# A merged run of small recurrence products in the second layer, and exponentials two steps later

## The chip, the cores and the metric

The kernel runs on one core of a Trainium2 chip. A core has five engines with their own instruction streams: TensorE (PE in the profile; its weight loads are PEld), VectorE (DVE), ScalarE (ACT), GpSimd (POOL) and SyncE (SP, which here only issues DMAs). The metric is the device time of one execution in microseconds, as a median of the runs.

## The reference

Two layers of a decoder trunk over 256 tokens of width 1024. Each layer projects the normalised tokens into ten groups of 512 columns, runs three branches, gates their outputs, and projects them back with a residual:

```python
for l in range(DEPTH):
    h = rms_norm(x, norm_g[l])
    q_a, k_a, v_a, q_h, f_h, i_h, q_m, z = jnp.split(h @ w_in[l], split_points, axis=-1)
    o_a = moba_attention(qa, ka, va)                      # 8 heads x 64, causal, own block of 256 keys
    o_h = hgrn2_chunkwise(q_h, f_h, i_h, lb_all[l])       # 4 heads x 128, gated linear recurrence
    o_m = memory_attention(qm, km, vm)                    # 4 heads x 128, over 256 memory tokens
    x = x + (jnp.concatenate([o_a, o_h, o_m], -1) * jax.nn.silu(z)) @ w_out[l]
```

The change touches the recurrence. Its score of query t on an earlier key s is a sum over 128 channels d of

```python
scores = jnp.einsum('bhtd,bhtsd,bhsd->bhts', qc, decay, kc)   # decay = product of the forget gates from s+1 to t
```

## The kernel before

**The stream of weights.** All projections are one chain of matmuls over 120 chunks of weights (128 x 1024 floats). A chunk is loaded by SP into `wr`, rounded on ScalarE into `wh` (L143), and the remainder `wr - wh` is formed on VectorE into `wl` (L158); each product is three matmuls (`wh` by the high part, `wh` by the low part, `wl` by the high part) into an `acc` bank. Loads run five chunks ahead of TensorE, `wh` four, `wl` two (`DMA_AHEAD`, `H_AHEAD`, `L_AHEAD`). Chunks of kind B give 12 matmuls of 512 columns, chunks of kind A 24 of 256 columns.

**The side work.** Everything else is written as generators (`g_...`), which `spawn` puts on a list. `slot`, called once per half chunk, advances each by one step; `yield n` makes one sleep n steps. Side work on TensorE writes to four `sd` banks, counted by `room`/`rel`. So the step number sets where an instruction stands in the program; a list scheduler of the framework then moves instructions within what data, buffers and pins allow. Each engine executes its own list in order.

**The recurrence (`g_hgrn`).** The decay of a pair (t, s) is built up in levels: level 1 pairs neighbours, level 2 pairs of two, then 4, 8, 16, 32, 64. For each channel a tree of forget products is kept (`Tm`, halved by `up`), queries `Q` and keys `K` are multiplied level by level by the forget products on their way to the middle of the pair (`mul`, L799), and the products of a level are then plain matmuls of 32 x 32 blocks, 32 of them, over the 128 channels. `row` issues such a run of 32 (L202): K block as weights, up to 48 columns of `QX` as moving operand, into one `sd` bank. Each product is fp32 and takes two passes, so a run of 32 is 64 records in the profile. Three runs are made for each layer: `low` (the diagonal and level 1, from `QX0`, `K0`), one for levels 2 and 4 (at m = 2) and one for levels 8 and 16 (at m = 8). `put` copies the parts of a bank that a level owns into `hSd` with a mask (`COPY_PREDICATED`, L796). Before, `low` is made beside the run of m = 2 and all use one pair of tiles, `QX` (`hQ`) and `K` (`hK`), which the next level overwrites in place. Levels 32 and 64 follow with runs of 16 and 8 products.

**The attention group.** `g_qk` transposes keys and queries (L993), casts them into `k2` (two tiles, with buffer tags `k2` and `y2`) and copies halves of them by DMA from ScalarE's queue (L1005). `g_moba_unit` (u = 0, 1) makes scores, maxima, sleeps four steps, takes exponentials on ScalarE (L1059, pinned in program order), scales them on VectorE (L1068), transposes `P` on TensorE (L1078, pinned) and copies it into `PT` (L1079). ScalarE's exponential and sigmoid are in different function sets: between them stands an `ACT_TABLE_LOAD`. Sigmoids `sg` of the gate (L732) come in the same part of the layer.

## Time and profile before

| | |
|---|---|
| median of 3 runs | 396.51 us (396.29 to 396.57) |
| the profiled execution | 396.15 us, span from first to last instruction 394.4 us |
| granted TensorE clock | 1.000 |
| VectorE and ScalarE busy | 315.3 us and 251.0 us |
| first layer's recurrence runs on TensorE | from 70.6 us on |
| second layer's, before the change | from 255.9 us on |
| DMA, mean | 180 GB/s |

A row of a timeline gives the start in us from the first instruction, the duration, the engine, the line, the operation with its output and input tiles, the shape, and how many alike stand in the row (x). On TensorE durations overlap, since matmuls are pipelined: the pace is read from start to start. `sd` and `acc` are PSUM banks. A row of a group (by line and form) gives the count, then the busy time in us, and the mean of one in ns. A row of waits gives who waited for whom: us in total, times, the longest.

### The profile page before, as it was taken

Reading aid. Unit: us, or ns where it says so; the run is one execution under the profiler, and the core shown is the slowest. Engines: PE = TensorE matmul, PEld = TensorE weight load, DVE = VectorE, ACT = ScalarE, POOL = GpSimd, SP = SyncE. Lnnn points to the kernel's source line nnn. Section 1 sums busy time; section 2 is a strip of 40 time slices with the busy share of each in tenths; the row PEclk is TensorE's granted clock in tenths of the full one; section 3 lists DMA queues with packets and bytes.
Section 4 is the critical chain, followed back from the end, with each engine's and each line's share of the span. In section 5 each row is a group of like instructions: output and inputs, shape, how many; then the busy total and the mean of one; then the engine's idle time right before and its main releaser. Section 6 shows DMA issues by size and latency. Waiting matters only on the chain.

```text
span 394.4 us, 7907 instructions
## 1 busy us (share of the span) xinstructions
PE 390.2 (99%) x3052; PEld 353.4 (90%) x3052; DVE 315.3 (80%) x628; ACT 251.0 (64%) x401; POOL 66.4 (17%) x94
## 2 busy tenths in 40 slices
PE   9999999999999999999999999999999999999996
PEld 6789988888999888999988999888889998899996
DVE  5799988999998748776586999799998684588563
ACT  6788776439687579644463785535865974968330
POOL 2007734430001002000061040033300200200000
DMA  8998654558544453533646375637665266444203
GB/s 274 419 349 303 198 198 144 162 158 234 197 161 157 165 191 131 157 111 111 209 161 212 124 237 181 209 108 227 193 193 172 73 197 200 140 158 161 81 27 108
DMA packets 22661, 70.92 MB, mean 180 GB/s; under 512 B 2528, under 2 KB 5984, under 8 KB 22624
## 3 DMA queue, kind: packets, MB, share of 16 engines
q1 hardware_dynamic: 19872, 67.86, 51.6%
q10 hardware_dynamic: 2752, 2.56, 2.4%
q8 instruction: 24, 0.39, 0.4%
q14 instruction: 13, 0.11, 0.1%
HBM read 67.27 MB, written 1.05 MB: 173 GB/s over the span
## 4 chain that ended last, share of the span: by engine, by line
PE 94%; DMA 3%; SPq 0%; ACT 0%; DVE 0%; POOL 0%; issue 0%; DVEq 0%; ACTq 0%
PE acc L198 60%; PE acc L1225 17%; PE sd L198 10%; DMA zT<-in_x_dram 2%; PE sd L202 2%; PE sd L1099 1%; PE sd L1078 1%; PE sd L993 1%; DMA mw<-in_front_dram 1%; PE sd L1187 1%; PE sd L633 0%; PE sd L1133 0%; PE sd L767 0%; SPq L123 0%; ACT sqx L446 0%; PE sd L423 0%
## 5 line engine op out<-in xcount | busy, mean ns | idle before, releaser
L143 ACT CAST wh<-wr 128x1024 fp32r<-128x1024 f32 x104 | 109.0, 1052 | 76.2 <-PE acc L198 44.2
L158 DVE TENSOR_TENSOR wl<-wr,wh 128x1024 fp32r<-128x1024 f32 x104 | 126.8, 1224 | 31.3 <-PE acc L198 11.3
L198 PE MATMUL acc<-wh,hT 128*128 128x512 f32 x384 | 120.5, 391 | 0.0
L198 PE MATMUL acc<-hT,wh 128*128 128x256 f32 x512 | 91.4, 280 | 0.0
L198 PEld LDWEIGHTS acc<-wh,hT 128*128 128x128 f32 x384 | 72.0, 188 | 14.7
L198 PEld LDWEIGHTS acc<-hT,wh 128*128 128x128 f32 x512 | 78.2, 188 | 0.2
L198 PE MATMUL acc<-wl,hT 128*128 128x512 f32 x192 | 75.5, 393 | 0.0
L198 PE MATMUL acc<-hT,wl 128*128 128x256 f32 x256 | 70.9, 279 | 0.0
L198 PEld LDWEIGHTS acc<-hT,wl 128*128 128x128 f32 x256 | 47.9, 188 | 0.1
L198 PEld LDWEIGHTS acc<-wl,hT 128*128 128x128 f32 x192 | 36.1, 188 | 7.3 <-DVE wl L158 0.2
L1225 PE MATMUL acc<-yh,wl 128*128 128x256 f32 x128 | 35.7, 280 | 0.0
L1225 PE MATMUL acc<-yl,wh 128*128 128x256 f32 x128 | 35.3, 277 | 0.0
L1225 PE MATMUL acc<-yh,wh 128*128 128x256 f32 x128 | 35.0, 278 | 0.0
L1225 PEld LDWEIGHTS acc<-yl,wh 128*128 128x128 f32 x128 | 24.1, 188 | 0.1
L1225 PEld LDWEIGHTS acc<-yh,wl 128*128 128x128 f32 x128 | 24.1, 188 | 0.0
L1225 PEld LDWEIGHTS acc<-yh,wh 128*128 128x128 f32 x128 | 23.8, 188 | 0.1
L161 DVE SCALAR_TENSOR_TENSOR wl<-wr,gT,wh 128x1024 fp32r<-128x1024 f32 (+1 forms) x14 | 18.8, 1355 | 4.9 <-PE acc L198 2.0
L1225 PE MATMUL acc<-y,wh 128*128 128x256 f32 x128 | 21.8, 276 | 0.0
L148 ACT ACTIVATE wh<-wr,gT 128x1024 fp32r<-128x1024 f32 (+1 forms) x14 | 15.2, 1089 | 10.4 <-PE acc L198 3.6
L1225 PEld LDWEIGHTS acc<-y,wh 128*128 128x128 f32 x128 | 19.2, 188 | 0.0
L1059 ACT ACTIVATE P<-P,nba,rq 128x128 f32<-128x128 f32 (+1 forms) x32 | 17.2, 539 | 0.9 <-DVE nba L1050 0.8
L1225 PE MATMUL acc<-y,wl 128*128 128x256 f32 x64 | 17.5, 276 | 0.0
(246 smaller groups left out, 669.3 us busy)
## 6 DMA issues: line engine op xcount, KB each, us to landing
wr<-in_w_in_dram SPq DMA_DIRECT2D x80, 512.0 KB, 3.7
wr<-in_w_out_dram SPq DMA_DIRECT2D x24, 512.0 KB, 3.2
wr<-in_w_mem_kv_dram SPq DMA_DIRECT2D x12, 512.0 KB, 3.4
k<-k ACTq DMA_DIRECT2D x8, 256.0 KB, 5.3
zT<-in_x_dram SPq DMA_DIRECT2D x2, 512.0 KB, 9.4
xs<-in_x_t_dram SPq DMA_DIRECT2D x2, 512.0 KB, 9.8
memr<-in_mem_dram SPq DMA_DIRECT2D x2, 512.0 KB, 4.9
mw<-in_front_dram SPq DMA_DIRECT2D x2, 384.0 KB, 4.8
```

The source lines that it names most:

```text
L143: ins = nc.scalar.copy(whs[i], raws[i])
L148: nc.scalar.activation(whs[i][:, sl], raws[i][:, sl], AF.Copy, scale=gT[:, g:g + 1])
L158: nc.vector.tensor_tensor(wls[i], raws[i], whs[i].bitcast(F32), op=OP.subtract)
L161: nc.vector.scalar_tensor_tensor(wls[i][:, sl], in0=raws[i][:, sl], scalar=gT[:, g:g + 1], in1=whs[i][:, sl].bitcast(F32), op0=OP.mult, op ...
L198: nc.tensor.matmul(o, lhsT=a, rhs=b, start=s, stop=e)
L202: tc.keep_in_program_order(nc.tensor.matmul(o, lhsT=a, rhs=b, start=True, stop=True))
L993: nc.tensor.transpose(pt[:, p * 128:(p + 1) * 128], kr[:, t, p * 128:(p + 1) * 128], ident)
L1059: pin(nc.scalar.activation(P[:, i, kc[t]], P[:, i, kc[t]], AF.Exp, bias=nb[:, c:c + 1], scale=rq[:, r:r + 1], accum_out=sm[:, c:c + 1]))
L1078: pin(nc.tensor.transpose(pt[:, i * 128:(i + 1) * 128], P[:, i, bs], ident))
L1099: pin(nc.tensor.matmul(po[w][rows, c + o:c + 256], lhsT=va[:, b, h * 64:(h + 1) * 64], rhs=PT[e][:, p, 256 * b:256 + 128 * b], start=b == ...
L1187: nc.tensor.transpose(pt[:, i * 256 + t * 128:i * 256 + (t + 1) * 128], P[:, t, i, b * 128:(b + 1) * 128], ident)
L1225: ins = nc.tensor.matmul(a, lhsT=wt, rhs=y, start=first and (to is not None or b % 2 == 0), stop=n == nk - 1 and j == 2, skip_group_check= ...
```

## The change

It touches the second layer (l = 1) alone.

1. In `g_hgrn`, queries and keys of levels 1 to 4 get tiles of their own, `hQ2` and `hK2`, in the buffers of tags `y2` and `k2`. At m = 2 no run is issued; the halves of keys and queries that the level leaves as they are go by two copies on ScalarE into `hK` and `hQ`, the others are multiplied into them. At m = 8, when three banks are free, the three runs (m = 8, m = 2, `low`) are issued together: 96 products, 192 passes. The masked writes of all three follow after that level's multiplications.
2. In `g_moba_unit`, the sleep ahead of the exponentials is 6 steps in place of 4, for both u.

The first layer goes through the same code with one run of `low` and m = 2, and one of m = 8, as before.

```diff
+        QX2, K2 = QX, K
+        if l:
+            QX2 = sb.tile([128, 32, 64], F32, name="hQ2", tag="y2", bufs=1)
+            K2 = sb.tile([128, 1024], F32, name="hK2", tag="k2", bufs=1)
+        Q2 = QX2[:, :, 0:32]
...
-        def up(m, src=K):
+        def up(m, src=K, dst=K):
...
-        nc.scalar.copy(pairs(K, 1)[:, :, 1], pairs(K0, 1)[:, :, 1])
+        nc.scalar.copy(pairs(K2, 1)[:, :, 1], pairs(K0, 1)[:, :, 1])
...
-        up(1, K0)
-        for m in (2, 8):
+        up(1, K0, K2)
+        first, todo = True, []
+        for m, QXm, Km in ((2, QX2, K2), (8, QX, K)):
+            todo.append((m, QXm, Km))
...
-            yield from room("sd", 2 if m == 2 else 1)
-            g, gs = row(K, lambda c: QX[:, c].rearrange("p (n x) -> p n x", x=4 * m)[:, :, m:])
-            if m == 2:
-                low = row(K0, lambda c: QX0[:, c])[1]
-            yield 2
...
+            rows = []
+            if m == 8 or not l:
+                yield from room("sd", len(todo) + first)
+                for n, a, k in todo[::-1]:
+                    rows.insert(0, (n, row(k, lambda c: a[:, c].rearrange("p (n x) -> p n x", x=4 * n)[:, :, n:])[1]))
+                todo = []
+                if first:
+                    low = row(K0, lambda c: QX0[:, c])[1]
+                yield 2
+                if first:
+                    rel("PTh")
+                    rel("PTl")
+                    put_low(low)
+                    rel()
+                first = False
+            else:
+                nc.scalar.copy(pairs(K, 2)[:, :, 1], pairs(K2, 2)[:, :, 1])
+                nc.scalar.copy(Qn[:, :, :, 0, 0], Qv[:, :, :, 0, 0])
+                yield 4
+            mul(Qn[:, :, :, 0, 1], Qv[:, :, :, 0, 1], Tq[:, :, :, 0, 0])
+            for v in range(2):
+                mul(Qn[:, :, :, 1, v], C[:, :, :, v], Tq[:, :, :, 0, 0])
+            up(m, Km)
+            up(2 * m)
+            for n, g in rows:
...
-        yield 4
+        yield (6 if l else 4)
```

Two places show what this does to the order.

TensorE, before, around the second layer's runs: first the run of m = 2 with `low`, where `hQ`, `hK` are the current tiles and `hQ_2965`, `hK_2814` are `QX0`, `K0`:

```order
L198 MATMUL acc<-wh,hT 128x512
L202 MATMUL sd<-hQ,hK 32x48 x32
L202 MATMUL sd<-hQ_2965,hK_2814 32x48 x32
L198 MATMUL acc<-wh,hT 128x512
L198 MATMUL acc<-wl,hT 128x512
```

and 56 matmuls of 512 columns later the run of m = 8, with eight transposes of keys behind it:

```order
L198 MATMUL acc<-wh,hT 128x512 x3
L202 MATMUL sd<-hQ,hK 32x48 x32
L993 MATMUL sd<-ident,kr 128x128 x8
L198 MATMUL acc<-wl,hT 128x512
L198 MATMUL acc<-wh,hT 128x512
```

After the change, 44 such matmuls behind the old place of the first run, `hQ_3055` and `hK_3056` being `hQ2` and `hK2`:

```order
L198 MATMUL acc<-wh,hT 128x512
L202 MATMUL sd<-hQ,hK 32x48 x32
L202 MATMUL sd<-hQ_3055,hK_3056 32x48 x32
L202 MATMUL sd<-hQ_2965,hK_2814 32x48 x32
L198 MATMUL acc<-wl,hT 128x512
L198 MATMUL acc<-wh,hT 128x512
L198 MATMUL acc<-wl,hT 128x512
L198 MATMUL acc<-wh,hT 128x512
L1009 MATMUL sd<-ident,kr 128x128 x4
L198 MATMUL acc<-wh,hT 128x512
```

The two runs have become one, and the transposes of keys come in two blocks of four, the first 8 matmuls ahead of the old place of the eight and the second 11 behind it.

ScalarE, before, around the exponentials of u = 0 in the second layer (`P,sma_3569`; `sq` is a square for the recurrence's output norm, `sg` a gate sigmoid, `wh` a weight chunk):

```order
L732 ACTIVATE sg<-acc 128x512
L1059 ACT_TABLE_LOAD
L1059 ACTIVATE P,sma_3569<-P,nba_3568,rq 128x256 x2
L589 ACTIVATE sq<-sd 128x512
L1059 ACTIVATE P,sma_3569<-P,nba_3568,rq 128x128 x2
L589 ACTIVATE sq<-sd 128x512
L1059 ACTIVATE P,sma_3569<-P,nba_3568,rq 128x128 x2
L143 CAST wh<-wr 128x1024 x2
L1059 ACTIVATE P,sma_3569<-P,nba_3568,rq 128x256 x2
L732 ACT_TABLE_LOAD
L732 ACTIVATE sg<-acc 128x512
```

And after, from the first `sq` on:

```order
L1075 ACT_TABLE_LOAD
L1075 ACTIVATE P,sma_3569<-P,nba_3568,rq 128x128 x2
L143 CAST wh<-wr 128x1024
L589 ACTIVATE sq<-sd 128x512
L1075 ACTIVATE P,sma_3569<-P,nba_3568,rq 128x128 x2
L1075 ACTIVATE P,sma_3569<-P,nba_3568,rq 128x256 x2
L143 CAST wh<-wr 128x1024
L732 ACT_TABLE_LOAD
L732 ACTIVATE sg<-acc 128x512
L143 CAST wh<-wr 128x1024
L1075 ACT_TABLE_LOAD
L1075 ACTIVATE P,sma_3569<-P,nba_3568,rq 128x256 x2
```

The last two exponentials now come behind a gate sigmoid and one more weight chunk, so the set of functions changes twice more. TensorE's transposes of this `P` move back by 35 matmuls of 256 columns. SP's and GpSimd's lists are unchanged.

## The prediction

> **What bounds the kernel now.** I read the page first, then the waits of TensorE alone, then the chain of waits, then the timelines of the second layer's recurrence.

> ```profile
> PE 390.2 (99%) x3052; PEld 353.4 (90%) x3052; DVE 315.3 (80%) x628; ACT 251.0 (64%) x401; POOL 66.4 (17%) x94
> PE 94%; DMA 3%; SPq 0%; ACT 0%; DVE 0%; POOL 0%; issue 0%; DVEq 0%; ACTq 0%
> ...
> PE sd L198 <- PEq L1361: 0.8, 1, 0.8
> PE sd L423 <- DVE dg L418: 0.2, 1, 0.2
> PE sd L198 <- ACT wh L148: 0.2, 1, 0.2
> ```

> TensorE is busy 99% of the span and 94% of the chain is its own. The lower three rows are all its waits: 1.2 us in 394.4, none on an operation that the change touches. So a gain must come out of TensorE's own stream, a loss must be a gap in it, and a microsecond taken from or given to another engine counts only where TensorE comes to wait for it.

> A busy TensorE is not always at its pace, so I need the pace. The chain of waits has two long unbroken stretches:

> ```profile
> 272.22 8.21 PE acc L198 x36
> ...
> 305.49 11.13 PE acc L198 x98
> ```

> That is 0.228 us for a matmul of 512 columns and 0.1136 us for one of 256. Against it the timeline shows what a run of small products costs at its edges:

> ```profile
> 255.58 0.39 PE L198 MATMUL acc<-wh,hT 128*128 128x512 f32 x1
> 255.90 1.57 PE L202 MATMUL sd<-hQ,hK 128*32 128x48 f32 x128
> 257.39 0.50 PE L198 MATMUL acc<-wh,hT 128*128 128x512 f32 x1
> 257.73 0.40 PE L198 MATMUL acc<-wl,hT 128*128 128x512 f32 x1
> ...
> 269.54 0.84 PE L198 MATMUL acc<-wh,hT 128*128 128x512 f32 x3
> 270.31 0.89 PE L202 MATMUL sd<-hQ,hK 128*32 128x48 f32 x64
> 271.13 1.09 PE L993 MATMUL sd<-ident,kr 128*128 128x128 f32 x8
> 271.98 0.48 PE L198 MATMUL acc<-wl,hT 128*128 128x512 f32 x1
> 272.29 0.40 PE L198 MATMUL acc<-wh,hT 128*128 128x512 f32 x1
> ...
> 285.36 0.63 PE L198 MATMUL acc<-wh,hT 128*128 128x512 f32 x2
> 285.82 0.60 PE L993 MATMUL sd<-ident,kr 128*128 128x128 f32 x4
> 286.18 0.48 PE L198 MATMUL acc<-wl,hT 128*128 128x512 f32 x1
> 286.49 0.63 PE L198 MATMUL acc<-wh,hT 128*128 128x512 f32 x2
> ```

> Each of the products leaves two records here (64 products, 128 records). From start to start, the matmul ahead of the first run takes 0.32 instead of 0.228 us and the one behind it 0.34: a run pays about 0.09 at its entry and 0.11 at its exit, besides its own records.

> **The change, part by part.**

> *The merged run (TensorE).* The first run with its edges: 257.73 - 255.58, less two matmuls at 0.228, is 1.69 us for 128 records. The second run has eight transposes behind it: its last matmul ahead starts at 269.54 + 2 x 0.228 = 270.00, so 272.29 - 270.00 - 0.456 = 1.83 us for both. Four transposes alone cost 286.49 - 285.59 (the second of two that begin at 285.36) - 0.456 = 0.44, eight 0.89, which leaves 0.94 us for 64 records. Now 192 records stand in one run. From the run's start to the next start the two take 257.39 - 255.90 = 1.49 and 271.13 - 270.31 = 0.82 us. The slope is (1.49 - 0.82) / 64 = 0.0105 us a record, so one run takes 1.49 + 64 x 0.0105 = 2.16, and with edges 0.09 + 0.11 it costs 2.36. Before it was 1.69 + 0.94 = 2.63: **-0.27 us**. The products themselves are the same ones.

> *Other neighbours on TensorE.* The transposes of keys and queries come as 4 and 4 where 8 stood, which costs nothing by the row above (0.44 a block of four). The next level's run of 32 records loses its transposes behind it and meets a 512-column matmul, whose exit of 0.11 it now pays in full; the blocks of scores are cut differently. Bounds: nothing, and one more exit, 0.11. I take 0.07, nearer the exit that the first run shows. Sum on TensorE: **-0.20 us**, with -0.27 and -0.16 as ends.

> *Two copies and two table loads on ScalarE.* The halves of keys and queries that level 2-4 leaves alone are copied. The nearest row for the keys is

> ```profile
> L834 ACT COPY hK<-hK 128x512 f32<-128x512 f32 x2 | 1.4, 687 | 0.5 <-DVE hK L694 0.5
> ```

> so 0.7 us, and for the queries, with half the elements, between 0.35 and 0.7. The later exponentials fall between the sigmoids of the gate, so the set of functions is switched two more times (the order shows 13 loads for 11) at 1.28 us. Together 3.7 us more on an engine that is busy 64% of the span: worth nothing unless it makes a consumer late. The place for that is the first half of the attention group's softmax:

> ```profile
> 303.02 0.59 ACT L732 ACTIVATE sg<-acc 128x512 f32<-128x512 f32 x1
> 303.62 1.28 ACT L1059 ACT_TABLE_LOAD   x1
> 304.92 0.60 ACT L1059 ACTIVATE P<-P,nba,rq 128x256 f32<-128x256 f32 x1
> ...
> 310.69 1.05 ACT L143 CAST wh<-wr 128x1024 fp32r<-128x1024 f32 x1 [0.68 <-ACT wh L143]
> ...
> 312.94 1.28 ACT L732 ACT_TABLE_LOAD   x1
> ...
> 314.72 1.04 ACT L143 CAST wh<-wr 128x1024 fp32r<-128x1024 f32 x1
> ...
> 314.94 0.20 DVE L1064 RECIPROCAL ria<-sma 128x8 f32<-128x8 f32 x1
> 315.18 1.93 DVE L1068 TENSOR_SCALAR P<-P,ria 128x128 f32<-128x128 f32 x8
> ...
> 316.46 0.60 PE L1078 MATMUL sd<-ident,P 128*128 128x128 f32 x4
> ```

> TensorE's transposes at 316.46 follow the first four scalings (about 316.0) by only 0.4 us. In the new order they stand 35 matmuls of 256 columns later (counted in it): 316.46 + 35 x 0.1136 - 0.2 = 320.2 is their new time. The new supply: cast 310.69 to 311.74, table 1.28 to 313.02, sigmoid 0.5 (from 312.94 + 1.28 to the cast at 314.72) to 313.5, cast to 314.6, table to 315.85, two exponentials at 0.6 to 317.05, reciprocal 0.25 to 317.3, now one weight remainder of 1.2 in front on VectorE to 318.5, four scalings 0.8 to 319.3. The margin grows from 0.4 to 0.9 us. If the second cast starts as late as before, 314.72, everything is 1.2 later, 320.5, and TensorE waits 0.3. I take 0 and keep +0.3.

> [...]

> *The burst on VectorE.* All ten conditional writes of the three runs now come after the muls of level 8-16, and no weight remainder (wl) stands among the first part of them.

> ```profile
> 270.95 1.22 DVE L158 TENSOR_TENSOR wl<-wr,wh 128x1024 fp32r<-128x1024 f32 x1
> ...
> 277.87 1.22 DVE L158 TENSOR_TENSOR wl<-wr,wh 128x1024 fp32r<-128x1024 f32 x1
> ...
> L799 DVE TENSOR_TENSOR hQ<-hQ,hT 128x256 f32<-128x256 f32 x12 | 4.5, 422 | 0.0
> L799 DVE TENSOR_TENSOR hK<-hK,hT 128x512 f32<-128x512 f32 x6 | 4.1, 688 | 0.0
> L590 DVE TENSOR_REDUCE ssa<-sq 128x8 f32<-128x512 f32 x4 | 2.7, 680 | 0.0
> L796 DVE COPY_PREDICATED hSd<-mk,sd 128x64 f32<-128x64 uint8 x6 | 1.3, 263 | 0.0
> L796 DVE COPY_PREDICATED hSd<-mk,sd 128x256 f32<-128x256 uint8 x1 | 0.4, 447 | 0.0
> ```

> The new stretch between two remainders: 2 reduces 1.36, 3 query muls 1.27, 2 key muls 1.38, 3 wide writes at most 0.447 each 1.34, 3 narrow ones 0.79, one key subtraction about as long as a key mul 0.69, two tiny scalings 0.3: 7.1 us of busy time. Before, the stretch from 270.95 to 277.87 held 7.5 by the same count (3 query muls, 2 key muls, two rotations and two key subtractions of about 0.69 each, four short products at 0.22, three writes, two tiny scalings), and TensorE did not wait then. Cost 0; without that cover, the excess over the remainders made two chunks ahead.

> *The keys' transfers.* Keys for the attention scores are written into the tiles that hQ2 and hK2 now hold, so their casts, subtractions and the four copies on ScalarE's DMA queue wait for the merged run. The second four transposes go 11 matmuls back, 2.3 us later by the pace above; the scores come 6 matmuls earlier, 1.4 us.

> ```profile
> 277.13 1.27 ACTq L1005 DMA_DIRECT2D k<-k  x2
> ...
> 288.59 0.74 PE L198 MATMUL sd<-k,yh 128*128 128x256 f32 x4
> ...
> DMA to landing us min/median/max: 3.2/4.7/7.0
> ```

> The first scores need the first two of those copies; with 277.13 and 4.7 us to land they had 6.8 us in hand, now about 3.1. Cost 0. SP's and GpSimd's order is unchanged, and the waits queued on SP behind weight loads stay where they were.

> **Sum.** The profiled execution took 396.15 us, 0.36 under the median of 396.51. -0.20 makes 395.95 of it, and **396.3 us** of the median.

> **Rivals.**

> *A, the switched tables come out dearer (slower).* Each extra load makes ScalarE lose another load's length, 1.28 us, on the path of the scalings: 319.3 + 2.56 = 321.9 against 320.2, so TensorE stands 1.7 us at the transposes, 396.5 - 0.2 + 1.7 = 398.0. It decides from 0.9 us on. Against it: 303.62 and 304.92 above. [...] 4%.

> *B, keys or weight remainders come late (slower).* The copies for the first scores are issued near 277.13 + 2.3 = 279.4 and needed at 288.59 - 1.4 = 287.2: a landing of over 7.8 us makes TensorE stand at the scores, where the longest of before took 7.0. What delays the issue (a key subtraction behind a remainder of 1.2 us on VectorE, more than once) comes on top. Priced at one such remainder, 1.2 us, it gives 396.5 - 0.2 + 1.2 = 397.5. 5%.

> *C, the run is not cheaper.* Three runs in a row into three banks keep their edges: 0, 396.5. The run of 128 records already spans two banks and two pairs of tiles and takes 1.49 us, less than twice the 0.82 of the run of 64, which speaks against it. 12%.

> *D, gain beyond the noise.* Edges twice as dear as read, with the neighbours following: -0.8 or more, 395.6. No row holds that much: 0.27 is all there is to save. 5%.

> **How the numbers follow.** Forecast 74%, C 12%, A 4%, B 5%, D 5%. About 0.2%, 0.8 us, is what a measurement here can tell from no change; the forecast and C lie inside, so same 0.86, faster 0.05, slower 0.09. The range takes the forecast with the ends of its terms (395.8: -0.27, one more exit of 0.11 saved, and the runs' own scatter of 0.3; 396.9: 396.3 with the 0.3 of the late cast and the scatter) and stretches up towards B: 395.8 to 397.2.

> **What would show it.** One row of 192 records in the second layer, lasting about 2.2 us, and no run of 64; the waits of TensorE still 1.2 us; the first transposes of P near 320.2 and the scalings ended before; 13 table loads. A wait of TensorE on the scalings (L1084 there) or on the keys makes me wrong upward; a run of 192 that lasts 2.4 us or more is C.

## The result and the profile after

| | before | after |
|---|---|---|
| median | 396.41 us (6 runs, 396.22 to 396.57) | 398.62 us (all 6 runs); 398.23 us (398.13 to 399.12) for the five that the ratio uses |
| profiled execution | 396.15 us, span 394.4 | 398.23 us, span 396.4 |
| ratio | | 1.0054 (95% interval 1.0043 to 1.0064) |

The sixth run of the changed kernel, 434.64 us at a mean granted clock of 0.852, is left out of the ratio. The change made the kernel slower by 0.5%; the forecast was 396.3 us, in a range of 395.8 to 397.2.

The page and the waits of TensorE in the kernel after (us in total, times, the longest), to be read beside the same rows of before:

```profile
PE 390.3 (98%) x3052; PEld 353.8 (89%) x3052; DVE 316.2 (80%) x628; ACT 254.8 (64%) x405; POOL 63.5 (16%) x94
...
PE sd L1009 <- DVE hK L804: 1.3, 1, 1.3
PE sd L198 <- PEq L1377: 0.8, 1, 0.8
PE sd L198 <- ACT wh L148: 0.5, 1, 0.5
PE acc L198 <- ACT wh L148: 0.3, 1, 0.3
```

TensorE's busy time is what it was (390.2 us). One long wait is new: 1.3 us at L1009, the transposes of keys, put down to a multiplication of keys on VectorE. The timeline of TensorE at that place:

```profile
265.57 0.39 PE L198 MATMUL acc<-wh,hT 128*128 128x512 f32 x1
265.89 2.25 PE L202 MATMUL sd<-hQ,hK 128*32 128x48 f32 x192
268.07 0.50 PE L198 MATMUL acc<-wl,hT 128*128 128x512 f32 x1
268.40 0.40 PE L198 MATMUL acc<-wh,hT 128*128 128x512 f32 x1
268.64 0.39 PE L198 MATMUL acc<-wl,hT 128*128 128x512 f32 x1
268.87 0.40 PE L198 MATMUL acc<-wh,hT 128*128 128x512 f32 x1
270.57 0.60 PE L1009 MATMUL sd<-ident,kr 128*128 128x128 f32 x4 [1.31 <-DVE hK L804]
```

The merged run itself behaves as forecast: from the matmul ahead to the run 0.32 us, the run 2.18, behind it 0.33. Four matmuls later TensorE stands: from 268.87 to 270.57 are 1.70 us where 0.23 is the pace, so **1.47 us are lost**.

Is VectorE late? The transposes read `kr`, and its last writer is in the timeline of VectorE:

```profile
264.59 0.68 DVE L994 TENSOR_TENSOR kr<-kr,rka 128x512 f32<-128x512 f32 x1
...
269.84 0.69 DVE L804 TENSOR_TENSOR hK<-hK,hT 128x512 f32<-128x512 f32 x1
```

`kr` was complete at 265.3, five microseconds ahead. The multiplication ends at 270.53, which is only the last event before TensorE goes on. TensorE's weight loads in the same stretch tell more:

```profile
268.87 0.14 PEld L1009 LDWEIGHTS sd<-ident,kr 128*128 128x128 f32 x1
270.58 0.36 PEld L1009 LDWEIGHTS sd<-ident,kr 128*128 128x128 f32 x3 [1.56 <-issue]
```

The first transpose's weight load, which reads `kr`, ran at 268.87, so `kr` was there. Then for 1.7 us came neither its matmul nor the next load. That is how it would look if TensorE had no instruction. The profile lists a queue q8 that it names instruction; here are its rows for the whole span and then for the 1.5 us from 267.8 to 269.3 (packets, MB, share):

```profile
q8 instruction: 24, 0.39, 0.4%
...
q8 instruction: 1, 0.02, 5.9%
```

**Theory F** (fetch), the author's: TensorE's instructions come in blocks, a packet each, estimated at 256 from the 254 and 256.4 above; the next block is asked for when one is begun, and is usable some 4 us later (estimated from the 3.9 below). By that the first instruction after the gap is the first of a block; counted back, the block before it has 9 records behind the merged run and 247 in it, so it begins 137 records (about 0.8 us) inside the run, at 266.7. Its own work ends at 269.1, after 2.4 us; the next block is there at 270.57, after 3.9. Before the change, the run of 128 passes had 256 instructions, and a block that began in it had most of its length in ordinary matmuls.

**Rival V**: TensorE waits for VectorE's multiplications, as the view of waits has it. **Rival L**: any run of 192 passes costs a drain. **Rival E**: the later exponentials cost it.

### The profile page after: what moved, and what is told of

Its sections match the earlier page's. It is cut to its first block, busy times and chain, and to the rows that moved or that the text cites. A ratio compares the mean times of both kernels' runs of the same rounds, so it can differ in the third digit from the quotient of the medians.

```text
span 396.4 us, 7913 instructions
## 1 busy us (share of the span) xinstructions
PE 390.3 (98%) x3052; PEld 353.8 (89%) x3052; DVE 316.2 (80%) x628; ACT 254.8 (64%) x405; POOL 63.5 (16%) x94
## 3 DMA queue, kind: packets, MB, share of 16 engines
q10 hardware_dynamic: 2752, 2.56, 2.6%
HBM read 67.27 MB, written 1.05 MB: 172 GB/s over the span
## 4 chain that ended last, share of the span: by engine, by line
PE 96%; DVE 1%; DMA 1%; issue 0%; SPq 0%; ACT 0%; DVEq 0%
PE acc L198 61%; PE acc L1241 17%; PE sd L198 11%; PE sd L1115 1%; PE sd L1094 1%; PE sd L202 1%; PE sd L1009 1%; PE sd L1203 1%; DMA wr<-in_front_dram 1%; PE sd L1149 0%; PE sd L767 0%; PE sd L633 0%; DVE wl L158 0%; DVE hK L804 0%; DVE ssa L590 0%; DVE hQ L804 0%
## 5 line engine op out<-in xcount | busy, mean ns | idle before, releaser
L143 ACT CAST wh<-wr 128x1024 fp32r<-128x1024 f32 x104 | 109.1, 1051 | 71.4 <-PE acc L198 39.1
L158 DVE TENSOR_TENSOR wl<-wr,wh 128x1024 fp32r<-128x1024 f32 x104 | 126.6, 1221 | 32.4 <-PE acc L198 11.0
L198 PE MATMUL acc<-wh,hT 128*128 128x512 f32 x384 | 121.6, 393 | 0.0
L198 PE MATMUL acc<-hT,wh 128*128 128x256 f32 x512 | 91.7, 281 | 0.0
L198 PEld LDWEIGHTS acc<-wh,hT 128*128 128x128 f32 x384 | 71.8, 188 | 14.4
L198 PEld LDWEIGHTS acc<-hT,wh 128*128 128x128 f32 x512 | 78.1, 188 | 0.2
L198 PE MATMUL acc<-wl,hT 128*128 128x512 f32 x192 | 75.6, 394 | 0.0
L198 PE MATMUL acc<-hT,wl 128*128 128x256 f32 x256 | 70.9, 279 | 0.0
L198 PEld LDWEIGHTS acc<-hT,wl 128*128 128x128 f32 x256 | 48.1, 189 | 0.0
L198 PEld LDWEIGHTS acc<-wl,hT 128*128 128x128 f32 x192 | 36.1, 188 | 7.2 <-DVE wl L158 0.2
L148 ACT ACTIVATE wh<-wr,gT 128x1024 fp32r<-128x1024 f32 (+1 forms) x14 | 15.2, 1089 | 11.2 <-PE acc L198 3.6
```

The lines of the kernel that those rows point to most:

```text
L143: ins = nc.scalar.copy(whs[i], raws[i])
L148: nc.scalar.activation(whs[i][:, sl], raws[i][:, sl], AF.Copy, scale=gT[:, g:g + 1])
L158: nc.vector.tensor_tensor(wls[i], raws[i], whs[i].bitcast(F32), op=OP.subtract)
L198: nc.tensor.matmul(o, lhsT=a, rhs=b, start=s, stop=e)
```

## The experiments

**Each part alone.** First the merged run with the exponentials as before the change:

```diff
-        yield (6 if l else 4)
+        yield 4
```

> The merged run alone: the exponentials sleep 4 steps again in both layers. Theory F (TensorE's instructions come in blocks of 16 KB, 256 weight loads and matmuls; the merged run uses one up before the next has arrived): the exponentials stand far behind the stall, so it stays, 1.3 to 1.5 us at the first transposes behind the run of 192, and the time is 398.0 to 398.6. Rival V (the transposes wait for VectorE's muls, as the view of waits has it): the same here. Rival E (the later exponentials cost it): the gap goes, 396.2 to 396.6.

Then the kernel before with the exponentials alone moved (`yield 4` to `yield (6 if l else 4)`):

> The kernel before with the exponentials of the second layer 6 steps behind instead of 4 and nothing else. Theory F: no run of 192, no stall, 396.3 to 396.9 (upper end if the 0.4 us that TensorE loses between 306 and 320 us to a slower pace of 256-column matmuls belongs to the exponentials). Rival V: 396.3 to 396.9 as well, VectorE has its old order. Rival E: 398 or more.

Measured: the merged run alone 399.04 us (398.73 to 399.40), ratio to before 1.0065 (1.0052 to 1.0078); the exponentials alone 396.81, ratio 1.0008 (0.9999 to 1.0017). The waits of TensorE with the merged run alone:

```profile
PE sd L1009 <- DVE msa L971: 1.1, 1, 1.1
PE sd L198 <- PEq L1377: 0.8, 1, 0.8
PE sd L198 <- ACT wh L148: 0.7, 1, 0.7
PE sd L1094 <- DVE P L1084: 0.6, 1, 0.6
```

Rival E falls: nearly all of the loss is the merged run's. The same gap is now put down to another instruction, a tiny scaling `msa`, which speaks against V. The time is 0.4 us above what was expected, and the transposes of `P` (L1094) now wait 0.6 us for the scalings, which fits: with the merged run the softmax comes late, and with the two steps more of sleep this wait is not there.

**Moving the blocks' limits, first try.** 13 or 30 more products in the first layer's level-64 run, whose results nobody reads:

```diff
             g = side_tile()
+            for _ in range(13 if l == 0 and m == 64 else 0):
+                mm_row(g[0:32, 480:512], K[:, 0:32], Q[:, 0])
```

> The changed kernel with 13 more products in the first layer's level-64 run; their results are read by nobody. They cost 13 x 2 records at about 0.0085 us, 0.2 us. Theory F: they move the blocks' limits by 52 records, from 137 records inside the merged run to 85, so that one whole block lies in the run; TensorE reaches its end 4 matmuls of 0.23 us earlier, the stall grows from 1.5 to 2.3 us or more and stands inside the run, ahead of its end; 399.2 to 399.8. Rival V (VectorE's muls) and rival L (any run of 192 records costs a drain of 1.5 us): stall unchanged, 398.4 to 398.8.

> The same with 30 more products, about 0.5 us. Theory F: the limit moves by 120 records, to 17 records inside the merged run; the sequencer crosses it some 50 records ahead of the matmuls, that is 16 or more matmuls of 0.23 us before the run begins, and the next block is there in time: no stall at the transposes, 398.4 - 1.5 + 0.5 = 397.4 (397.0 to 397.7), faster than with 13. Rivals V and L: the stall stays, 398.8 to 399.1.

Measured with 13: 401.59 us (399.99 to 402.26), above what any theory gave (the last section has a reason). The profiled execution was the shortest, and TensorE's timeline there shows the gap where F puts it, inside the run:

```profile
266.51 2.06 PE L202 MATMUL sd<-hQ,hK 128*32 128x48 f32 x171
271.06 0.45 PE L202 MATMUL sd<-hQ,hK 128*32 128x48 f32 x21 [2.48 <-issue]
...
272.48 0.60 PE L1011 MATMUL sd<-ident,kr 128*128 128x128 f32 x4
```

The profile finds nothing that TensorE waited for between these two passes of the run; it says "issue". The transposes no longer wait. 21 matmuls of the run and four of the stream lie between the gap and the transposes: the 26 passes that were added, but for one. The one is made up by two semaphore instructions: ahead of the gap TensorE's trace has 25 of them here and 27 after the change.

With 30 the time was 403.13 us, where F gave 397.4. No wait at the run was left, but another had come, in the first layer:

```profile
PE sd L198 <- ACT hK L923: 1.9, 1, 1.9
```

The added products had also changed the order in which the scheduler put other instructions of all three busy engines, so neither time is a clean test. The next three change no order.

**Moving the limits alone.** The program starts with 18 warming matmuls of 256 columns, while the first weights are on their way. The same columns in fewer or more instructions shift every later block; the list of every engine is otherwise the same:

```diff
-    one = nc.const_aps.tensor(1.0, [128, 256], BF)
+    one = nc.const_aps.tensor(1.0, [128, 512], BF)
     pt = side_tile()
-    for _ in range(WARM):
-        mm(pt[:, :256], one[:, :128], one, True, True)
+    for _ in range(9):
+        mm(pt[:, :512], one[:, :128], one, True, True)
```

> The changed kernel, with the 18 warming matmuls of 256 columns at the program's start as 9 of 512: the same columns, 18 fewer records (a weight load and a matmul each), nothing else moves. Theory F: every block's limit falls 18 records later in the program, 155 instead of 137 records inside the merged run, so 9 more matmuls of 0.227 us stand between the run's end and the block's: 2.0 us against a stall of 1.5. The stall goes: 396.5 to 397.1. Rivals V (VectorE's muls) and L (any run of 192 records costs a drain): unchanged, 398.2 to 398.8.

With widths `[512] * 4 + [256] * 10`:

> The same with 4 of 512 and 10 of 256 columns: 8 records fewer, 4 more matmuls of 0.227 us behind the run in its block, 0.9 us. Theory F: a stall of 0.4 to 0.7 us is left, 397.2 to 397.9, between the other two. Rivals V and L: 398.2 to 398.8.

With widths `[256] * 15 + [16] * 29`:

> The same with 15 warming matmuls of 256 columns and 29 of 16: 52 records more. Theory F: the limit lies 85 records inside the run, a whole block lies in it, TensorE stands 2.3 to 2.8 us inside the run; 399.2 to 400.2 (more if the small ones at the start end later than the first weights arrive, which the profile's first 5 us would show). Rivals V and L: 398.2 to 398.8.

| records | wait in the profiled execution | where | median, us |
|---|---|---|---|
| -18 | none | | 397.19 (396.77 to 398.72) |
| -8 | 2.1 us | 8 records later than after the change | 398.53 (397.28 to 400.95) |
| +52 | 2.9 us | inside the run, 22 passes ahead of its end | 400.56 (399.42 to 402.91) |

The profiled execution with 8 fewer is the slowest of its eight, 400.95 us; the last section says why.

TensorE's waits with 18 records fewer: the wait at the transposes is gone.

```profile
PE sd L198 <- PEq L1377: 0.8, 1, 0.8
PE sd L198 <- ACT wh L148: 0.5, 1, 0.5
```

With 8 fewer, the gap stands four matmuls further on, behind the transposes:

```profile
269.46 0.60 PE L1009 MATMUL sd<-ident,kr 128*128 128x128 f32 x4
272.20 0.59 PE L198 MATMUL acc<-wh,hT 128*128 128x512 f32 x1 [2.14 <-issue]
272.58 0.63 PE L198 MATMUL acc<-wl,hT 128*128 128x512 f32 x1
```

Four transposes and the first load of the next matmul: 8 instructions, the 8 that were taken away at the start, 265 us earlier. And with 52 more:

```profile
266.96 2.06 PE L202 MATMUL sd<-hQ,hK 128*32 128x48 f32 x170
271.96 0.46 PE L202 MATMUL sd<-hQ,hK 128*32 128x48 f32 x22 [2.94 <-issue]
```

The place of the gap follows the count of instructions to the record, through transposes, a weight load and the middle of a run. Counted from the program's start, the gap always stands behind the same matmul, the 2130th. These rows reach from the start into the gap, after the change, with 8 fewer and with 52 more (stretch, length, busy time and instructions of TensorE, weight loads, VectorE, ScalarE and GpSimd, granted clock, DMA share, GB/s):

```profile
0.00:270.50 270.50, 267.70 (x2130) 240.55 (x2131) 226.49 (x448) 176.62 (x267) 55.53 (x88) 1.00 0.59 198
0.00:272.15 272.15, 269.12 (x2130) 241.17 (x2131) 227.29 (x451) 177.43 (x268) 56.60 (x88) 1.00 0.57 196
0.00:271.90 271.90, 268.01 (x2130) 240.91 (x2131) 226.51 (x448) 176.29 (x267) 55.91 (x88) 1.00 0.58 197
```

V and L, which hold it at the transposes or at the run, fall. The size of the gap did not follow with 8 fewer: F gave 0.4 to 0.7 us and the profiled execution had 2.1; the median, 398.53, is 0.6 above the top of F's range. By F's count of 256, from the first instruction of a block to the first of the next it took 3.9 us after the change, 5.1 with 8 fewer and 4.5 with 52 more. The instruction queue shows which part varies. The packet landed at 269.27, 270.86 and 270.57 in these three, and TensorE went on 1.3 to 1.4 us later each time (270.57, 272.20, 271.96). But the packet started 1.2, 2.1 and 2.2 us after the block had begun. What delays its start (the weights that are loaded at the same time are the nearest thing) was not tried.

**The low run at its own place.** The run of `low` goes where the first run stood before the change:

```diff
-                yield from room("sd", len(todo) + first)
+                yield from room("sd", len(todo) + (first and not l))
...
-                if first:
+                if first and not l:
                     low = row(K0, lambda c: QX0[:, c])[1]
...
             else:
+                yield from room("sd")
+                low = row(K0, lambda c: QX0[:, c])[1]
```

> The changed kernel with the run of low and level 1 issued at its own place, about 36 matmuls ahead of the run of m = 2 and m = 8, which is then 128 records long. Theory F: the block's limit lies about 50 records inside the run of 128, and 25 matmuls of 512 columns follow the run inside the block: no stall, 396.4 to 397.1. Rival V: the muls and writes keep nearly their order, the transposes wait as before, 398 or more. Rival L: a shorter run drains sooner, 397 to 398.

Measured: 397.24 us (396.57 to 397.75), ratio to before 1.0015 (1.0006 to 1.0024), a little above F's range, and no gap in its profile. A run of 128 passes does no harm at that place. This alone would not part F from L; the shifts above do.

**The changed kernel again, and 120 records more.** On one chip: the changed kernel, the one with 18 records fewer, and one with widths `[256] * 9 + [16] * 69`.

> The changed kernel once more, on one chip with the next two, to compare them without a change of chip. Theory F: 398.2 to 399.2, with a stall of 1.3 to 2.4 us at the first transposes behind the merged run, long where the fetch took long. All rivals: the same.

> The kernel with 9 warming matmuls of 512 columns once more (18 records fewer ahead of the run). Theory F: no wait at the transposes, 1.2 to 1.8 us under the changed kernel of the same call. Rivals V and L: the same time as that.

> The changed kernel with 9 warming matmuls of 256 columns and 69 of 16: 120 records more, the order on every engine otherwise unchanged. Theory F, with the sequencer some 50 to 60 records ahead of the matmuls: the limit lies 17 records inside the run, the next block is asked for some 20 matmuls of 0.227 us (4 us or more) before the run begins and is there in time; no stall, although 26 more matmuls gave 2.9 us. 396.8 to 397.5, and up to 0.8 more if the 69 small ones at the start end after the first weights are there. Theory F without that lead: a stall of 2 us or more, 399 or more. Rivals V and L: as the changed kernel, 398.2 to 399.2.

Measured: 398.56 us (397.93 to 398.82), 397.19 (396.77 to 398.40) and 398.19 (398.03 to 398.90). The changed kernel has its 1.3 us wait again, the other two have none at the transposes. 18 instructions fewer at the start save 1.4 us of the median. In the profiled execution with 18 fewer a small rest of the gap is left, nine matmuls behind its old place, where F puts the limit: behind the 2130th matmul the step is 0.52 us, where 0.23 is the pace.

```profile
271.14 0.39 PE L198 MATMUL acc<-wl,hT 128*128 128x512 f32 x1
271.66 0.63 PE L198 MATMUL acc<-wh,hT 128*128 128x512 f32 x2
```

With 120 more, TensorE has a single wait, at the start:

```profile
PE sd L198 <- PEq L1377: 0.8, 1, 0.8
```

Its run begins at 267.27, and the instruction packet, which with 52 more started at 269.6, inside the gap, starts in the stretch from 265.4 to 267.4:

```profile
q8 instruction: 1, 0.02, 5.5%
```

So it started ahead of the run or in its first 0.13 us, where those of the three traces with a gap started 1.2 to 2.2 us after the block had begun. That it was asked for some 50 to 60 records ahead of the matmuls is the author's estimate, which no run shows as such. The packet that starts at 248.90 after the change has 3721 records ahead of it, about 28 short of the limit two blocks before the gap (4261 - 512 = 3749). All but 0.17 us of the gap is gone (from the run's start to the next matmul's, 2.35 us instead of 2.18), though more instructions were added than in the case with the longest gap. The waits are 0 to 0.3 us at -18, 2.1 at -8, 1.3 at 0, 2.9 at +52 and 0.2 at +120. The median is 0.7 us above F's range without the start and within it with the allowance of 0.8 us for the 69 small matmuls there. The trace bears that out: the first layer's run of 128 passes begins at 71.74 us here and at 71.07 and 71.17 in the other two.

No version beat the kernel before: the best with the whole merged run, 18 records fewer, stands at 1.0017 (1.0008 to 1.0026), the one with the low run at its own place at 1.0015.

## Why the prediction was wrong

**What bounds the kernel: right in the main.** TensorE's busy time did not move, and the larger part of the loss is a gap in its stream. But a loss need not be a gap, as the prediction had it: a smaller part is a slower pace of its matmuls (below).

**The merged run: its cost right, what follows it missing.** It was to cost 2.36 us with its edges and did: 0.09 + 2.18 + 0.11 = 2.38, so the slope of 0.0105 us a record held. The step that failed is that the sum on TensorE ends with the run's exit and the waits were to stay at 1.2 us: a run of 192 passes was priced as if the instructions behind it were always there. This term was put at nothing without a reason, and no rival asked where instructions come from. In its place the profiled execution shows a gap of 1.47 us four matmuls behind the run, where, by theory F, the next block of instructions was late. The longest run in the trace of before has 256 instructions, and it shows no such gap; the rate could have been seen in it (256 instructions in 1.49 us against 29 us in the stream), and the instruction queue's 24 packets stand on its page.

In the stream of large matmuls a block's limit costs no wait that the profile shows (before, 24 packets, and TensorE's waits are 1.2 us in all, the longest, 0.8, at the start); with the merged run it costs from nearly nothing (0.2 us with 120 records more) to a wait of 2.9 us (with 52 more), depending on where the limit falls.

**TensorE's other pieces: a second term was missing.** Without the gap (18 records fewer) the change is still 0.7 us slower, not 0.2 faster: 0.9 us are missing. The chain of waits shows half of it: before, 98 matmuls of 256 columns took 11.13 us from 305.49, 0.1136 each; after, the like stretch reads

```profile
309.42 13.08 PE acc L198 x111
```

0.1178 each, 0.47 us more for 111. The changed kernel, when run again, and all shifted versions had the same 13.08 us there; the exponentials alone did not bring it. But the order of instructions alone does not set the pace: in the first layer, which the change doesn't touch, the changed kernel and the one with the exponentials at 4 steps have, over the same 129 matmuls,

```profile
27.62 14.83 PE acc L198 x129
...
27.40 15.51 PE acc L198 x129
```

0.7 us apart. What sets it, and why it followed the merged run in the second layer, stays open, as do the other 0.4 us. Two places where some of these may lie: the start, since in the profiled execution with 18 fewer the first layer's run already begins 0.35 us later than before (70.85 against 70.50); and the exponentials, since alone they measured 0.35 us above before, which could not be told from no change.

**ScalarE: right, for a reason that was only half seen.** The transposes of `P` came at 322.34 (1.9 us of the 2.1 beyond the forecast are the gap and the slower pace) and didn't wait. There are 13 loads of function sets, as read from the order. The load ahead of the late exponentials:

```profile
315.53 1.04 ACT L143 CAST wh<-wr 128x1024 fp32r<-128x1024 f32 x1
316.59 1.28 ACT L1075 ACT_TABLE_LOAD   x1
317.88 0.60 ACT L1075 ACTIVATE P<-P,nba,rq 128x256 f32<-128x256 f32 x1
```

It starts as the cast ends, at 316.57, and the exponential follows it after 1.29 us. As before the change (sigmoid's end at 303.61, exponential at 304.92), the switch takes its load of 1.28 us and at most 0.03 more, and rival A fell. That the exponentials had to move because of the merged run (0.6 us of wait without it) was not in the prediction.

**The burst on VectorE and the keys' transfers: right.** TensorE waited for neither; the row that names VectorE is the gap of 1.47 us, by theory F the fetch. Rival B fell. C and D fell with the size of the run, which was as read.

## What to carry to other kernels

Count instructions, not only time: here a run of 384 instructions in 2.2 us came to a gap, by theory F because a block, estimated at 256 of them, was used up before the next was there (by that count 3.9 to 5.1 us from one block's first instruction to the next one's, in three traces with a gap). Whether there is one depended on where the block's limit fell, which 8 and 18 records fewer and 52 and 120 more at the start moved. So a long run of tiny matmuls may do better broken by ordinary ones, as the low run at its own place did, and a change there is judged by several shifts of it. And a wait in the profile whose named releaser wrote nothing that the waiting instruction reads is a sign to look at the weight loads and the instruction queue.

## What the hardware showed besides

The same gap had three names: two different VectorE instructions when it fell on the transposes, and "issue" when it fell behind them or inside a run.

After the gap with 8 records fewer, the granted clock halved for 3.4 us (a mean of 0.50 in the second row; the columns are the stretch, its length, busy time and instructions of TensorE, weight loads, VectorE, ScalarE and GpSimd, the granted clock, DMA share and GB/s):

```profile
269.90:272.10 2.20, 0.16 (x2) 0.08 (x1) 2.13 (x7) 0.58 (x1) 1.74 (x1) 0.99 0.22 82
272.10:275.50 3.40, 3.30 (x8) 2.59 (x8) 2.29 (x6) 0.55 (x1) 2.40 (x4) 0.50 0.03 7
275.50:278.90 3.40, 3.40 (x18) 2.79 (x17) 2.68 (x6) 1.90 (x3) 0.00 (x0) 1.00 0.46 154
```

That costs TensorE about another 1.7 us (half of 3.4), so this gap of 2.1 us cost nearly twice its length. The mean granted clock of that execution is 0.995. The longer gap with 52 more records brought no such stretch in its profiled execution; two of the other five, 401.18 and 402.91 us, have a mean of 0.996, which one such stretch would give. So have three of the five with 13 more products, 401.59 us and above; the other two, 399.99 and 400.16 at a mean of 1.000, are 0.2 to 0.4 above F's range. What decides which gaps are followed by such a stretch was not shown: the 2.1 us with 8 fewer were, the 2.9 us with 52 more were not.
